# Dilated heads: the second score product contracts over 128 partitions instead of 64

## The chip, the cores and the metric

The kernel runs on one core of a Trainium2 chip. The metric is the device time of one execution in microseconds (us). Before the change three runs gave a median of 1386.52 us (1386.37 to 1387.81).

## What is computed

Two layers of a bidirectional encoder over 512 tokens of width 1024. Each layer mixes tokens with 16 heads of width 64: 4 differential heads, 6 dilated heads and 6 two-dimensional neighbourhood heads; their outputs go through an output projection, then a gated conv-MLP. The part that the change touches is the score of the dilated heads:

```
s = jnp.einsum('...nqd,...nkd->...nqk', qb, kb).astype(jnp.float32) * (DH ** -0.5)
s = jnp.where(mask, s, NEG)
```

The kernel computes all 512 x 512 scores of a head at once and puts the three dilation patterns into one additive table.

## The kernel before

Matrix products run in a 32-bit format (`F32R`) of reduced precision. For full precision a tensor is split into a rounded part `hi` and a remainder `lo`, and a projection is three products, hi*hi + lo*hi + hi*lo (`mm3`, lines 482 to 485; the value projections do the same on lines 684 to 686). Weights come from HBM as `raw` tiles (line 329), ScalarE (ACT) casts `hi` (line 351), and GpSimd (POOL) or VectorE (DVE) subtracts to get `lo` (line 353). Three such weight units fit during attention.

For a pair of dilated heads the rotary step writes hi and lo of q and k to a scratch tensor in HBM, and `dil_stack` (line 645) loads them back, stacked on the partitions, by seven DMAs of the SP queue (lines 651 to 657):

- `K[:, hh]`: 64 partitions hold k hi, 64 hold k lo (hi is the lower half for head 0 of the pair, the upper half for head 1)
- `Q[:, hh]`: q hi on both halves
- `L`: q lo of head 0 on partitions 0 to 63, q lo of head 1 on partitions 64 to 127

`dil_step` (line 931) computes a block of 128 queries of one head. Line 938 is a product over all 128 partitions, q hi with k hi plus q hi with k lo. Line 939 adds q lo with k hi: a product over 64 partitions only, `L[lr]` with `K[lr]`. Then DVE adds the table and takes the row minimum of the negated scores (line 942), ACT takes the exponential (line 947), DVE the reciprocal (line 951), ACT scales (line 952), TensorE (PE) transposes in four pieces (line 813, `tr` in `tr_stage`), ACT and DVE split the transposed block (lines 817 and 821), and PE multiplies with the values (lines 834 and 836). The differential heads run before them: their scores are line 902, DVE row maxima line 904, the combination of two probability blocks line 920, and they share lines 813 to 847. In layer 0 DVE also computes the modulation vectors (line 411), one row of weights at a time.

What sets the order: `attention_phase` runs a loop in which a generator (`proj`) emits two products' worth of projection at a time, a clock (`ck`) starts the later stages of the steps after given lags, and a credit counter lets a new step in. On top of that the framework's scheduler orders each engine's instructions by its own estimates when the program is built, so that a change of one shape can move neighbours. On the chip every engine runs its list in order.

There are 6 heads x 4 blocks x 2 layers = 48 executions of `dil_step`, so 48 products of line 938 and 48 of line 939.

Of the kernel before, what the change touches and what calls it, by code (L numbers as in the profile page):

```python
# [13 lines left out]
F32R = mybir.dt.float32r  # L14
# [8 lines left out]
S = 512  # L23
# [150 lines left out]
def build(ctx, tc, a):  # L174
    nc = tc.nc
    V, A, G, PE, SY = nc.vector, nc.scalar, nc.gpsimd, nc.tensor, nc.sync
# [11 lines left out]
    def uid():  # L188
        cnt[0] += 1
        return cnt[0]  # L190
# [4 lines left out]
    def tmp(shape=(128, 512), dt=F32, tag="tmp", bufs=TMP_BUFS):  # L195
        return wp.tile(list(shape), dt, tag=tag, bufs=bufs, name=f"{tag}{uid()}")
# [106 lines left out]
    def take(tag, shape=(128, 512)):  # L303
        assert av[tag] > 0, tag
        av[tag] -= 1
        return tmp(shape) if tag == "tmp" else ps(tag, shape)

    def give(tag):
        av[tag] += 1
# [258 lines left out]
    def attention_phase(l, gen, fest):  # L568
# [7 lines left out]
        def at(shape, dt, tag, bufs):  # L576
            return ap.tile(list(shape), dt, tag=tag, bufs=bufs, name=f"{tag}{uid()}")

        def mark(lag, *keys):
            ck.after(lag, lambda: ready.update(keys))  # L580
# [64 lines left out]
        def dil_stack(p):  # L645
            sv = scr["b", p].rearrange("(q v) r n -> q r v n", q=2)
            K = at([128, 2, S], F32R, "ks", 2)
            Q = at([128, 2, S], F32R, "qs", 2)
            L = at([128, S], F32R, "ql", 2)
            Kf, Qf, Lf = K.bitcast(F32), Q.bitcast(F32), L.bitcast(F32)  # L650
            SY.dma_start(Kf[:, 0], sv[1, :, 0])
            SY.dma_start(Kf[0:64, 1], sv[1, 64:128, 1])
            SY.dma_start(Kf[64:128, 1], sv[1, 0:64, 1])
            SY.dma_start(Qf[0:64], sv[0, 0:64])
            SY.dma_start(Qf[64:128], sv[0, 0:64])
            SY.dma_start(Lf[0:64], sv[0, 64:128, 0])
            SY.dma_start(Lf[64:128], sv[0, 64:128, 1])
            stk["b", p] = (K, Q, L)
            mark(2, ("b", p))

# [136 lines left out]
        def tr_need(st, qb):  # L797
            if qb % 2 == 0:
                return {"pt": 1, "ph": 1}
            return {"pt": 1, "if": lambda: ("ph", qb // 2) in st}  # L800

        def tr_stage(st, qb, P_of):
            half = qb // 2

            def tr():
                if ("ph", half) not in st:
                    av["ph"] -= 1
                    st["ph", half] = at([128, 4, 256], F32R, "ph", 2)
                    st["pl", half] = at([128, 4, 256], F32R, "pl", 2)
                pt = take("pt", (128, 4, 128))  # L810
                P = P_of()
                for kt in range(4):
                    PE.transpose(pt[:, kt], P[:, kt * 128:kt * 128 + 128], ident)  # L813
                give("tmp")
                st["pt", qb] = pt
                sl = slice((qb % 2) * 128, (qb % 2) * 128 + 128)
                A.copy(st["ph", half][:, :, sl], pt)  # L817

            def lo():
                sl = slice((qb % 2) * 128, (qb % 2) * 128 + 128)  # L820
                V.tensor_tensor(out=st["pl", half][:, :, sl], in0=st["pt", qb],  # L821
                                in1=st["ph", half][:, :, sl].bitcast(F32), op=ALU.subtract)
                st["lo", qb] = True
                give("pt")

            return tr, lo

        def av_half(st, half, vt, hidx, c, hh, fin):
            if half == 0:
                st["o"] = take("o")  # L830
            o = st["o"]
            oh = o[:, half * 256:half * 256 + 256]
            for kt in range(4):
                PE.matmul(oh, vt[:, kt, hidx, :], st["ph", half][:, kt], start=(kt == 0), stop=False)
            for kt in range(4):
                PE.matmul(oh, vt[:, kt, hidx, :], st["pl", half][:, kt], start=False, stop=(kt == 3))
            give("ph")
            if half == 1:
                if c not in of:
                    of[c] = at([128, S], F32, "of", 5)  # L840
                t = tmp()
                dst = slice(64 * hh, 64 * hh + 64)
                oth = slice(64 - 64 * hh, 128 - 64 * hh)
                A.copy(t[dst], o[oth])

                def s1():
                    V.tensor_tensor(out=of[c][dst], in0=o[dst], in1=t[dst], op=ALU.add)
                    give("o")
                    if fin:
                        fin()  # L850

                ck.after(1, s1)
# [78 lines left out]
        def dil_step(hd, qb, st):  # L931
            p, hh = divmod(hd, 2)
            K, Q, L = stk["b", p]
            lr = slice(64 * hh, 64 * hh + 64)
            nm = tmp((128, 2), tag="sm2", bufs=24)
            s = take("s")
            sl = slice(qb * 128, qb * 128 + 128)
            PE.matmul(s, Q[:, hh, sl], K[:, hh], start=True, stop=False)
            PE.matmul(s, L[lr, sl], K[lr, hh], start=False, stop=True)  # L939
            P = take("tmp")  # L940
            e0 = OFF_T + 384 - 128 * qb
            V.tensor_tensor_reduce(out=P, in0=s, in1=cst[:, e0:e0 + S], op0=ALU.add, op1=ALU.min, scale=1.0,
                                   scalar=3e38, accum_out=nm[:, 0:1])
            give("s")

            def s1():
                A.activation(out=P, in_=P, func=AF.Exp, bias=nm[:, 0:1], scale=-1.0, accum_out=nm[:, 1:2])

            def s2():
                r = tmp((128, 2), tag="sm2", bufs=24)  # L950
                V.reciprocal(out=r[:, 0:1], in_=nm[:, 1:2])
                A.activation(out=P, in_=P, func=AF.Copy, scale=r[:, 0:1])

            tr, lo = tr_stage(st, qb, lambda: P)
            stages = [(1, {}, s1), (1, {}, s2), (2, tr_need(st, qb), tr), (1, {}, lo)]
            if qb % 2 == 1:
                fin = (lambda: ready.add("b_done")) if hd == HB - 1 else None
                stages.append((2, {"o": int(qb == 1), "if": lambda: ("lo", qb - 1) in st and (qb == 1 or "o" in st)},
                               lambda: av_half(st, qb // 2, vs["vb"], hd, 2 + p, hh, fin)))
            ck.chain(*stages)  # L960
# [88 lines left out]
        for hd in range(HB):  # L1049
            st = {}  # L1050
            if hd % 2 == 0:
                stacks.append((("scr", ("b", hd // 2)), 4 * HD + 4 * hd - (4 if hd == 0 else 8),
                               lambda hd=hd: dil_stack(hd // 2)))
            steps += [(1.5, {"s": 1, "tmp": 1}, (("b", hd // 2), "vb"),
                       lambda hd=hd, qb=qb, st=st: dil_step(hd, qb, st)) for qb in range(4)]
# [266 lines left out]

# [12 lines left out]
```

## Time and profile before

| what | value |
|---|---|
| median of 3 runs | 1386.52 us |
| span of the profiled execution | 1383.9 us |
| PE busy (x instructions) | 1328.0 us, 96% (x6992) |
| DVE busy | 896.2 us, 65% |
| ACT busy | 608.2 us, 44% |
| POOL busy | 177.8 us, 13% |
| chain that ended last: PE, DVE, DMA | 85%, 8%, 3% |
| mean busy share of 16 DMA engines | q1 46.3%, q10 0.4% |

The profiled execution has a span of 1383.9 us from the first to the last instruction; its own device time is not listed apart, and the median of the timed runs stands 2.6 us above the span. Matmuls are pipelined: the length that a row gives for one is the time until its last result, so what a matmul costs in a full queue is the distance from its start to the start of the next.

### The profile page before, as it was taken

Reading aid. Unit: us, or ns where it says so; the run is one execution under the profiler, and the core shown is the slowest. Engines: PE = TensorE matmul, PEld = TensorE weight load, DVE = VectorE, ACT = ScalarE, POOL = GpSimd, SP = SyncE. Lnnn points to the kernel's source line nnn. Section 1 sums busy time; section 2 is a strip of 40 time slices with the busy share of each in tenths; the row PEclk is TensorE's granted clock in tenths of the full one; section 3 lists DMA queues with packets and bytes.
Section 4 is the critical chain, followed back from the end, with each engine's and each line's share of the span. In section 5 each row is a group of like instructions: output and inputs, shape, how many; then the busy total and the mean of one; then the engine's idle time right before and its main releaser. Section 6 shows DMA issues by size and latency. Waiting matters only on the chain.

```text
span 1383.9 us, 18577 instructions
## 1 busy us (share of the span) xinstructions
PE 1328.0 (96%) x6992; PEld 1109.3 (80%) x6992; DVE 896.2 (65%) x1615; ACT 608.2 (44%) x1051; POOL 177.8 (13%) x116
## 2 busy tenths in 40 slices
PE   5887899999999999999998989999999999999997
PEld 4785678779988888888898867877898888888886
DVE  7968976977776666656675697466576434443443
ACT  3336487645543233223342667775445322332331
POOL 3732321003000000000113232200200000000002
PEclk9999999999999999999999999999999999999998
DMA  9565564644466666665523645142334323333211
GB/s 365 164 182 150 162 208 142 197 134 149 124 195 181 202 180 184 198 196 165 175 76 108 178 140 171 57 126 77 97 98 124 103 94 91 96 102 92 79 44 61
DMA packets 69262, 196.16 MB, mean 142 GB/s; under 512 B 7602, under 2 KB 12850, under 8 KB 69044
## 3 DMA queue, kind: packets, MB, share of 16 engines
q1 hardware_dynamic: 68448, 193.10, 46.3%
q10 hardware_dynamic: 724, 1.87, 0.4%
q8 instruction: 55, 0.90, 0.3%
q14 instruction: 35, 0.29, 0.1%
HBM read 180.78 MB, written 14.16 MB: 141 GB/s over the span
## 4 chain that ended last, share of the span: by engine, by line
PE 85%; DVE 8%; DMA 3%; POOL 2%; issue 1%; ACT 1%; POOLq 0%; SPq 0%; DVEq 0%; ACTq 0%
PE pr L483 12%; PE pr L485 12%; PE pr L484 11%; PE s L484 5%; PE s L485 5%; PE s L483 5%; PE pt L484 4%; PE pt L485 4%; PE pt L483 4%; PE pt L813 2%; PE o L485 2%; PE o L483 2%; PE o L484 2%; PE o L1027 2%; PE s L939 1%
## 5 line engine op out<-in xcount | busy, mean ns | idle before, releaser
L351 ACT CAST whi<-raw 128x1024 fp32r<-128x1024 f32 (+2 forms) x144 | 135.0, 938 | 268.8 <-PE pr L485 103.4
L353 DVE TENSOR_TENSOR wlo<-raw,whi 128x1024 fp32r<-128x1024 f32 (+2 forms) x101 | 111.2, 1101 | 94.9 <-ACT whi L351 94.1
L444 POOL TENSOR_TENSOR tmp<-tmp,tmp 128x256 f32<-128x256 f32 (+1 forms) x38 | 36.7, 966 | 892.5 <-ACT tmp L442 891.2
L351 ACT CAST fhi<-raw 128x1024 fp32r<-128x1024 f32 (+1 forms) x76 | 74.9, 985 | 143.9 <-PE pr L485 53.7
L411 DVE CUSTOM_DVE_ANT_0 tmp<-raw,cb,par 128x1024 bf16<-128x1024 f32 x80 | 106.8, 1336 | 41.6 <-DMA raw<-w_ada 41.5
L485 PE MATMUL pr<-h,whi 128*128 128x512 f32 (+1 forms) x330 | 121.9, 374 | 8.0 <-POOL h L479 7.6
L483 PE MATMUL pr<-h,whi 128*128 128x512 f32 (+1 forms) x330 | 125.9, 382 | 1.6 <-DVE tmp L596 0.7
L353 POOL TENSOR_TENSOR wlo<-raw,whi 128x768 fp32r<-128x768 f32 (+1 forms) x43 | 96.0, 2238 | 243.2 <-ACT whi L351 215.6
L484 PE MATMUL pr<-h,wlo 128*128 128x512 f32 (+1 forms) x330 | 123.1, 373 | 1.0 <-POOL wlo L353 1.0
L353 DVE TENSOR_TENSOR flo<-raw,fhi 128x1024 fp32r<-128x1024 f32 (+1 forms) x76 | 87.4, 1150 | 55.2 <-ACT fhi L351 54.4
L483 PE MATMUL pr<-h,fhi 128*128 128x512 f32 (+1 forms) x244 | 86.7, 357 | 0.0
L484 PE MATMUL pr<-h,flo 128*128 128x512 f32 (+1 forms) x244 | 86.5, 356 | 0.0
L485 PE MATMUL pr<-h,fhi 128*128 128x512 f32 (+1 forms) x244 | 85.5, 357 | 0.5 <-DVE h L479 0.5
L485 PEld LDWEIGHTS pr<-h,whi 128*128 128x128 f32 x330 | 62.1, 190 | 19.8 <-POOL h L479 9.5
L483 PEld LDWEIGHTS pr<-h,whi 128*128 128x128 f32 x330 | 62.7, 190 | 16.0 <-issue 4.1
L484 PEld LDWEIGHTS pr<-h,wlo 128*128 128x128 f32 x330 | 63.1, 191 | 9.7 <-POOL wlo L353 1.2
L1157 ACT ACTIVATE tmp<-tmp 128x512 f32<-128x512 f32 x44 | 27.6, 631 | 94.3 <-DVE tmp L1152 77.4
L821 DVE TENSOR_TENSOR pl<-pt,ph 128x512 fp32r<-128x512 f32 x80 | 54.4, 686 | 14.7 <-ACT ph L817 14.5
L904 DVE TENSOR_REDUCE sm<-s 128x1 f32<-128x512 f32 x64 | 43.0, 682 | 28.4 <-PE s L902 28.0
L813 PE MATMUL pt<-cst,tmp 128*128 128x128 f32 x320 | 48.6, 274 | 13.3 <-DVE tmp L920 11.0
L817 ACT CAST ph<-pt 128x512 fp32r<-128x512 f32 x80 | 46.7, 586 | 32.3 <-PE pt L813 31.2
L477 ACT ACTIVATE h<-tmp,mod,gsc 128x256 fp32r<-128x256 f32 (+1 forms) x58 | 35.3, 621 | 53.3 <-DVE tmp L474 52.5
(265 smaller groups left out, 3657.3 us busy)
## 6 DMA issues: line engine op xcount, KB each, us to landing
raw<-w SPq DMA_DIRECT2D x132, 512.0 KB
raw<-w_ada SPq DMA_DIRECT2D x80, 512.0 KB
raw<-w SPq DMA_DIRECT2D x72, 384.0 KB
araw<-w_ada SPq DMA_DIRECT2D x16, 512.0 KB
raw<-w SPq DMA_DIRECT2D x16, 320.0 KB
ks<-nab SPq DMA_DIRECT2D x12, 384.0 KB
scr0b<-nat SPq DMA_DIRECT2D x12, 256.0 KB
scr1b<-nat SPq DMA_DIRECT2D x12, 256.0 KB
```

Source lines behind the costliest of these rows:

```text
L351: A.copy(hi, r)
L353: (G if on_pool else V).tensor_tensor(out=lo, in0=r, in1=hi.bitcast(F32), op=ALU.subtract)
L411: V.tensor_tensor_reduce(out=junk, in0=r, in1=cb, op0=ALU.mult, op1=ALU.add, scale=1.0, scalar=par[:, OFF_B + l * 48 + j:OFF_B + l * 48 + ...
L444: self.last = self.eng.tensor_tensor(out=self.sq[0][:, sl], in0=self.sq[0][:, sl], in1=self.sq[m][:, sl], op=ALU.add)
L477: ins = A.activation(out=hi, in_=t, func=AF.Identity, scale=A_col, bias=sh_col)
L483: PE.matmul(out, wh, hh, start=first, stop=False)
L484: PE.matmul(out, wl, hh, start=False, stop=False)
L485: return PE.matmul(out, wh, hl, start=False, stop=last)
L813: PE.transpose(pt[:, kt], P[:, kt * 128:kt * 128 + 128], ident)
L817: A.copy(st["ph", half][:, :, sl], pt)
L821: V.tensor_tensor(out=st["pl", half][:, :, sl], in0=st["pt", qb], in1=st["ph", half][:, :, sl].bitcast(F32), op=ALU.subtract)
L904: V.tensor_reduce(out=nm[:, m:m + 1], in_=s, axis=AX.X, op=ALU.max, negate=True)
```

## The change

`L` becomes as large as `Q`: q lo of both heads, stacked twice on the partitions. Line 656 and line 657 load 64 partitions x 2 heads x 512 each, twice the bytes of before (256 KB instead of 128 KB per DMA). The second product takes all 128 partitions of `L` and `K`, so it adds q lo with k hi and also q lo with k lo, which was left out before. The scratch that the framework keeps for descriptors of DMAs issued by POOL shrinks to 4096, which leaves room for the larger `L`. One line is gone, so lines behind 934 have numbers lower by one in the changed kernel: its two products are lines 937 and 938, and the DVE step is line 941.

```
@@ -646,15 +646,15 @@
-            L = at([128, S], F32R, "ql", 2)
+            L = at([128, 2, S], F32R, "ql", 2)
...
-            SY.dma_start(Lf[0:64], sv[0, 64:128, 0])
-            SY.dma_start(Lf[64:128], sv[0, 64:128, 1])
+            SY.dma_start(Lf[0:64], sv[0, 64:128])
+            SY.dma_start(Lf[64:128], sv[0, 64:128])
@@ -931,12 +931,11 @@
-            lr = slice(64 * hh, 64 * hh + 64)
...
-            PE.matmul(s, L[lr, sl], K[lr, hh], start=False, stop=True)
+            PE.matmul(s, L[:, hh, sl], K[:, hh], start=False, stop=True)
@@ -1322,7 +1321,7 @@
-    nc = bacc.Bacc("TRN2", target_bir_lowering=False, num_devices=1)
+    nc = bacc.Bacc("TRN2", target_bir_lowering=False, num_devices=1, dynamic_dma_scratch_size=4096)
```

The scheduler moves a few instructions. On PE all moves lie in layer 0; in layer 1 PE's order is the same as before. Three places matter below.

The first is PE in layer 0, where the sixth dilated step (score `s_1800`) stands among products of a projection (`pr_1772`). `pt_1781` is the transpose of the third step. Before:

```order
L485 MATMUL pr_1772<-h_275,whi_1529 128x512
L938 MATMUL s_1800<-ks_1330,qs_1331 128x512
L939 MATMUL s_1800<-ks_1330,ql_1332 128x512
L483 MATMUL pr_1772<-h_311,whi_1529 128x512
L484 MATMUL pr_1772<-h_311,wlo_1530 128x512
L485 MATMUL pr_1772<-h_312,whi_1529 128x512
L483 MATMUL pr_1772<-h_352,whi_1529 128x512
L834 MATMUL o_1811<-ph_1694,vb_791 128x256 x4
L813 MATMUL pt_1781<-cst,tmp_1686 128x128 x4
```

And in the changed kernel, from a point nine projection products later:

```order
L485 MATMUL pr_1772<-h_394,whi_1529 128x512
L937 MATMUL s_1800<-ks_1330,qs_1331 128x512
L938 MATMUL s_1800<-ks_1330,ql_1332 128x512
L483 MATMUL pr_1772<-h_434,whi_1529 128x512
L834 MATMUL o_1811<-ph_1694,vb_791 128x256 x4
L836 MATMUL o_1811<-pl_1695,vb_791 128x256
L813 MATMUL pt_1781<-cst,tmp_1686 128x128 x4
```

The sixth step's scores, and with them the products with the values and the transpose of the third step, come behind more projection products (those of `h_352`, `h_353`, `h_393` and `h_394`) than before.

The second is DVE in layer 0, in the last differential steps, just ahead of the first dilated step. `tmp_1448` is what PE's transpose `pt_1535` reads; in the difference:

```order
 L904 TENSOR_REDUCE sm_1499<-s_1501 128x1
 L919 SCALAR_TENSOR_TENSOR sm_1491<-sm_1491,sm_1156,nl_735 128x1
+L904 TENSOR_REDUCE sm_1499<-s_1505 128x1
+L920 SCALAR_TENSOR_TENSOR tmp_1448<-tmp_1448,sm_1491,tmp_1444 128x512
+L821 TENSOR_TENSOR pl_1473<-pt_1474,ph_1472 128x4x128
 L411 ISA tmp_1495,mod_99<-raw_1387,cb,par 128x1024
 L411 ISA mod_99 128x1
-L920 SCALAR_TENSOR_TENSOR tmp_1448<-tmp_1448,sm_1491,tmp_1444 128x512
-L904 TENSOR_REDUCE sm_1499<-s_1505 128x1
-L821 TENSOR_TENSOR pl_1473<-pt_1474,ph_1472 128x4x128
 L847 TENSOR_TENSOR of_1488<-o_1370,tmp_1489 64x512
```

The modulation row (line 411) goes behind the three instructions that PE and ACT wait for; the work in this stretch is the same.

The third is the SP queue in layer 1, at the load of the second pair of dilated heads (`ks_7797`, `qs_7798`, `ql_7799`); `raw_7872` is a weight unit of 768 columns:

```order
-L329 DMA raw_7872<-w 128x768
+L653 DMA ks_7797<-scr1b_7575 64x512
 L651 DMA ks_7797<-scr1b_7575 128x512
 L652 DMA ks_7797<-scr1b_7575 64x512
-L653 DMA ks_7797<-scr1b_7575 64x512
 L654 DMA qs_7798<-scr1b_7575 64x2x512
 L655 DMA qs_7798<-scr1b_7575 64x2x512
-L656 DMA ql_7799<-scr1b_7575 64x512
-L657 DMA ql_7799<-scr1b_7575 64x512
+L656 DMA ql_7799<-scr1b_7575 64x2x512
+L657 DMA ql_7799<-scr1b_7575 64x2x512
+L329 DMA raw_7872<-w 128x768
```

The weight unit now stands behind the seven loads of the stack instead of ahead of them.

## Rows read from the trace of the kernel before

**Rows 1.** Page, part 1: busy time and share of PE, PE's weight loads, and the others

```profile
PE 1328.0 (96%) x6992; PEld 1109.3 (80%) x6992; DVE 896.2 (65%) x1615; ACT 608.2 (44%) x1051; POOL 177.8 (13%) x116
```

**Rows 2.** PE's waits, whole span: who waited for whom; total, times, longest (us)

```profile
PE pt L813 <- DVE tmp L920: 11.0, 9, 1.9
```

**Rows 3.** Windows: length, busy us (count) of each engine, PE's granted clock, DMA share, GB/s

```profile
130.00:172.00 42.00, 35.43 (x179) 26.78 (x178) 41.23 (x67) 22.49 (x47) 13.82 (x6) 1.00 0.51 142
172.00:250.00 78.00, 78.00 (x420) 62.10 (x421) 55.48 (x132) 61.01 (x117) 13.82 (x7) 1.00 0.56 166
250.00:706.00 456.00, 455.66 (x2338) 381.30 (x2336) 315.52 (x546) 171.90 (x272) 22.44 (x22) 1.00 0.58 174
832.00:848.00 16.00, 16.00 (x79) 11.76 (x78) 15.43 (x31) 11.59 (x23) 2.84 (x1) 1.00 0.59 174
```

**Rows 4.** Lines 938 and 939: count, ns min/median/max, first and last start, shapes

```profile
L938 PEld LDWEIGHTS s<-ks,qs x48: 186/188/192, 166.6 to 913.3; 128*128 128x128 f32 x48
L938 PE MATMUL s<-ks,qs x48: 387/397/505, 166.8 to 913.5; 128*128 128x512 f32 x48
L939 PE MATMUL s<-ks,ql x48: 491/492/502, 167.1 to 913.8; 64*128 64x512 f32 x48
```

**Rows 5.** PE's timeline at a dilated step among projections: start us, length us

```profile
244.73 0.40 PE L938 MATMUL s<-ks,qs 128*128 128x512 f32 x1
245.06 0.49 PE L939 MATMUL s<-ks,ql 64*128 64x512 f32 x1
245.48 0.50 PE L483 MATMUL pr<-h,whi 128*128 128x512 f32 x1
245.82 0.39 PE L484 MATMUL pr<-h,wlo 128*128 128x512 f32 x1
246.05 0.40 PE L485 MATMUL pr<-h,whi 128*128 128x512 f32 x1
```

**Rows 6.** PE's timeline, a step behind transposes and ahead of value projections

```profile
206.69 0.48 PE L938 MATMUL s<-ks,qs 128*128 128x512 f32 x1
207.10 0.50 PE L939 MATMUL s<-ks,ql 64*128 64x512 f32 x1
207.53 0.45 PE L684 MATMUL pr<-whi,h 128*128 128x384 f32 x1
207.81 0.34 PE L685 MATMUL pr<-wlo,h 128*128 128x384 f32 x1
207.99 0.35 PE L686 MATMUL pr<-whi,h 128*128 128x384 f32 x1
```

**Rows 7.** PE's timeline, a transpose that waited, then full-array products

```profile
171.98 0.63 PE L813 MATMUL pt<-cst,tmp 128*128 128x128 f32 x4 [0.44 <-DVE tmp L920]
172.37 0.48 PE L484 MATMUL pr<-h,wlo 128*128 128x512 f32 x1
172.69 0.39 PE L485 MATMUL pr<-h,whi 128*128 128x512 f32 x1
```

**Rows 8.** ACT's timeline, layer 1: scaling of the second dilated step (line 952)

```profile
843.32 0.69 ACT L952 ACTIVATE tmp<-tmp,sm 128x512 f32<-128x512 f32 x1
```

**Rows 9.** PE's timeline, layer 1: first and fourth step, transposes of the second

```profile
832.58 0.39 PE L938 MATMUL s<-ks,qs 128*128 128x512 f32 x1
...
841.37 0.39 PE L938 MATMUL s<-ks,qs 128*128 128x512 f32 x1
...
844.53 0.60 PE L813 MATMUL pt<-cst,tmp 128*128 128x128 f32 x4
```

**Rows 10.** Window at the border of the two layers, columns as in Rows 3

```profile
758.00:764.60 6.60, 5.31 (x17) 5.31 (x18) 1.24 (x2) 0.83 (x1) 0.51 (x2) 0.50 0.78 235
```

**Rows 11.** Timeline of POOL and DVE in layer 0, ahead of the dilated steps

```profile
160.12 2.64 POOL L353 TENSOR_TENSOR wlo<-raw,whi 128x1024 fp32r<-128x1024 f32 x1 [9.54 <-ACT whi L351]
160.46 2.85 DVE L920 SCALAR_TENSOR_TENSOR tmp<-tmp,sm,tmp 128x512 f32<-128x512 f32 x1
```

**Rows 12.** Line 656 on the SP queue, layer 1: issue ns, first and last start

```profile
L656 SPq DMA_DIRECT2D ql<-scr1b x3: 603/605/612, 814.0 to 861.2; - x3
```

## The prediction

> **What bounds the kernel now.** First the busy shares of the page: PE is busy 96% of the span, DVE 65%, ACT 44% [rows 1]. A share says little about a single stage, so next PE's waits: the longest of them in total is the transpose of a differential step waiting for DVE, 11.0 us in 9 waits [rows 2]. It shows that DVE does end PE's waits somewhere. The windows show where [rows 3]: in 130 to 172 us, the differential steps of layer 0 and the first dilated ones, DVE is busy 41.23 of 42.00 us and PE only 35.43; in 172 to 250, where the rest of layer 0's dilated steps stand, PE is busy all 78.00 us and DVE 55.48. Layer 1 begins in the same way: DVE 15.43 of 16.00 in 832 to 848. Behind layer 0's steps PE goes on without a break, 455.66 of 456 us. So time taken from PE's list in the dilated steps comes off the end, except where DVE, not PE, sets the pace; that is the case in the first steps of each layer.
>
> Then the two products themselves. Line 939 takes 492 ns in the median, line 938 only 397, though the first feeds half as many partitions and both stream 512 columns [rows 4]. The cost in a full queue is the distance from start to start, and there the whole effect is to be seen [rows 5]. From 938 to 939 it is 0.33 us, from 939 to the next product 0.42, from that to the one behind it 0.34; after that the full-array products go on at 0.23. Not only the 64-row product is dear: the one ahead and the one behind it pay too. All three have 128 columns of weights and a free result buffer, and no engine is named as a releaser in these rows. What differs is the shape 64*128 between two of 128*128.
>
> **The change, part by part.** *The product of line 939 becomes full-array.* Now, among projections, three products take 245.82 - 244.73 = 1.09 us [rows 5]. All full-array they should take 3 x 0.23 = 0.69 us, the pace of the last two rows there. That is 0.40 us less. Behind transposes and ahead of value projections the three take 207.81 - 206.69 = 1.12 us [rows 6]. Without the 64-row one I put 0.32 us for the first (a full-array product behind transposes, 172.37 to 172.69 [rows 7]), 0.23 for the second and 0.18 for a value product of 384 columns (207.81 to 207.99 [rows 6]): 0.73 us, 0.39 less. These two patterns agree, so I take 0.39 us for each of the 48 steps [rows 4]: 18.7 us off PE's list. It is a price by subtraction: no row shows the changed product itself, but the one ahead of it, line 938, has its shape, its kind of operands and 397 ns. From below the bound is nothing (the gaps stay, second rival), from above 0.40 x 48 = 19.2 us.
>
> Here a page speaks against the change. The Trainium skill, "TensorE: Matmul & The Clock Gate", section "Why this matters for your kernels", has a single product with a short contraction take the same time as a full one, the gain of small ones lying only in running several at once. By that rule widening the contraction changes nothing and the sum is 0 instead of 18.7 us; the trace does not agree, with 492 ns against 397 for the same 512 columns [rows 4].
>
> *What DVE keeps back.* In layer 0 two dilated steps stand ahead of the transpose at 171.98, which waits for DVE's line 920 [rows 7]. DVE is full up to there [rows 3], so what PE saves in these two it waits longer: 2 x 0.39 = 0.8 us lost. The next two steps' transposes have waits of their own to fear, since DVE also feeds the dilated steps, but the third step's transpose now stands behind the sixth step's scores and more projection products, which fill the time. I take nothing more there. In layer 1 PE's order is unchanged. The transpose of the second step starts at 844.53, and its input is done at 843.32 + 0.69 = 844.01: a slack of 0.52 us [rows 8, 9]. Four steps stand ahead of it (832.58 to 841.37), and they save 4 x 0.39 = 1.56 us; if DVE's chain stands still, 1.56 - 0.52 = 1.0 us of that becomes a wait. Bounds: nothing lost (DVE's chain moves along), or all of the first eight steps of both layers, 16 x 0.39 = 6.2 us.
>
> *The moved DVE and PE instructions in layer 0.* Line 920 for `tmp_1448` and two others go ahead of a modulation row. That may remove a PE wait near 163 us, but DVE's work up to the wait at 171.98 is the same, and that wait takes up what was won. I count 0. Its bound as a loss is one collision: line 920 there is stretched to 2.85 us beside a subtraction of POOL of 2.64 us [rows 11], so a DVE instruction that meets POOL at a bad moment can lose up to 2.6 us; as a gain the bound is the same, if the collision that is there now goes away.
>
> *Six pairs of loads twice as large.* Each stack brings 2 x 128 KB more, 262 KB, six stacks 1.6 MB. At the mean of 142 GB/s in that stretch [rows 3] 262 KB take 1.8 us. Issue on the SP queue is 0.6 us for the small load [rows 12], and I take the same for the large one, since the number of instructions stays. What hides it: in layer 1 the first `L` is issued at 814.0 us and the first product starts at 832.58, 18 us later [rows 12, 9]. If that cover were gone, PE would wait up to 1.8 us at each of six stacks. In layer 1 a weight unit moves behind seven loads of a stack; weights are fetched three units ahead, a unit is 24 projection products of 0.23 us or 5.5 us without the attention products between them, so some 16 us ahead. I count 0. The smaller descriptor scratch I count at nothing as well: no row of the trace shows a DMA issued by POOL, for which it is kept. The extra q lo times k lo comes free in the same pass.
>
> *The clock.* At the border of the layers, 758.0 to 764.6, the granted clock is 0.50, the 1.2 GHz level, and PE is busy only 5.31 of 6.60 us [rows 10]. At full clock this would take half, so such a stretch costs 2.6 us. In the stretches around the dilated steps it is 1.00, the 2.4 GHz level [rows 3]. Layer 1 starts some 8 us earlier now; whether the stretch stays is open, so 2.6 us goes into the range on either side. I count 0.
>
> **Sum.** 18.7 - 0.8 - 1.0 = 16.9 us. Against the profiled span: 1383.9 - 16.9 = 1367.0. The median of the runs lies 2.6 us above that span, so I give 1386.5 - 16.9 = **1369.6 us**.
>
> **Rivals.** *First, DVE holds on longer.* If it keeps back all of the first eight steps of each layer, 18.7 - 6.2 = 12.5 us remain: 1374.0. For it speaks DVE's full window [rows 3] and the collisions with POOL [rows 11], which a faster PE may set off elsewhere, as it frees weight buffers sooner; against it that from 172 us on PE is full and DVE has 22 us to spare.
>
> *Second, the shape is not the cause.* Then the three distances stay, and the time stays at 1386.5. For it: the trace has no other 64-row product of 512 columns to compare. Against it: no row without a 64-row product beside it shows 0.42 us, and the row ahead and the row behind both pay, which a slow read of `L` would not explain.
>
> *Third, slower: weight loads of the same rows come into the open.* A load takes 188 ns [rows 4]. If it could not run under a product of the same rows, each of the three products would cost 0.19 + 0.23 = 0.42 us, 48 x 3 x 0.42 = 60.5 us against 48 x 1.1 = 52.8 now: 7.7 us slower, 1394.2. It decides from 0.13 us of open load for each product on, where three cost 1.09. Against it: full-array products follow one another at 0.23 us [rows 5] with loads of 0.19, which leaves no room for an open load. The Trainium skill, "TensorE: Matmul & The Clock Gate", section "The mechanism", does say that a weight load overlaps with a product under way only when the row groups differ; by that rule this rival would come true, and the trace does not agree (0.23 us from start to start [rows 5]).
>
> **How the numbers follow.** The forecast has 0.74, from 1365.2 us (18.7 us and a vanished slow stretch, 1386.5 - 18.7 - 2.6) to the first rival's 1374.0. The first rival has 0.16, up to 1374.0 + 2.6 = 1376.6. Second rival, or the gain lost by something not seen here: 0.05. Third: 0.03. Below 1365.2: 0.02. The range is 1365.2 to 1376.6 and leaves out about 0.1 to 0.15. A measurement of this kernel can tell 0.2%, 2.8 us, from no change. Faster: 0.74 + 0.16 + 0.02 = 0.92; the same: 0.05; slower: 0.03.
>
> **What would show it.** The second product (line 938 in the changed kernel) with shape 128*128 and a median near 397 ns; from start to start 0.23, 0.23 and 0.23 us in the three, 0.32 for the first behind transposes. PE's total busy time down by 15 us or more; PE full and DVE at two thirds or more in the dilated steps. PE waits at the transposes of the first steps of each layer, some 1 us each in total. The prediction is wrong if the distances stay above 0.3 us, if new waits for DVE or ACT in the dilated steps sum to over 5 us, or if a wait for `ql` or `raw` shows up.

## The result, and the profile after

The changed kernel takes **1370.68 us** in the median of 4 runs (1368.71 to 1373.33), beside 1387.11 for the kernel before on the same chip. The ratio is 0.9886, with a 95% interval of 0.9874 to 0.9898; of 1386.52 us that is 15.8 us less, the gain that this text goes by (the two medians above are 16.4 us apart). Run once more, word for word, it gave 1368.82 us and 0.9883 (0.9868 to 0.9897). 0.9886 x 1386.5 is 1370.7, with the interval 1369.0 to 1372.4; the forecast was 1369.6, in a range of 1365.2 to 1376.6. The profiled execution has a span of 1370.5 us (1372.36 us as a run), 13.4 us under the span before.

Busy time by engine (page of the changed kernel, part 1), against [rows 1]:

```profile
PE 1310.2 (96%) x6992; PEld 1108.9 (81%) x6992; DVE 896.2 (65%) x1615; ACT 605.5 (44%) x1051; POOL 179.4 (13%) x116
```

PE has lost 17.8 us of busy time with the same number of instructions; DVE's is the same to the tenth. The two products by line (count, ns min/median/max, first and last start), against [rows 4]:

```profile
L938 PE MATMUL s<-ks,ql x48: 388/392/477, 168.1 to 901.2; 128*128 128x512 f32 x48
```

492 ns have become 392. The same step among projections, on PE's timeline, against [rows 5]:

```profile
240.38 0.39 PE L937 MATMUL s<-ks,qs 128*128 128x512 f32 x1
240.61 0.40 PE L938 MATMUL s<-ks,ql 128*128 128x512 f32 x1
240.84 0.39 PE L483 MATMUL pr<-h,whi 128*128 128x512 f32 x1
241.07 0.40 PE L484 MATMUL pr<-h,wlo 128*128 128x512 f32 x1
```

and one ahead of value projections and behind a transpose, against [rows 6]:

```profile
205.47 0.60 PE L813 MATMUL pt<-cst,tmp 128*128 128x128 f32 x4
205.82 0.48 PE L937 MATMUL s<-ks,qs 128*128 128x512 f32 x1
206.14 0.40 PE L938 MATMUL s<-ks,ql 128*128 128x512 f32 x1
206.97 0.41 PE L684 MATMUL pr<-whi,h 128*128 128x384 f32 x1 [0.44 <-DVE nat L738]
```

From start to start the first shows 0.23 us three times where 0.33, 0.42 and 0.34 stood, 0.69 us in place of 1.09; the second shows 0.32 where 0.41 stood. The last row of the second is a sign of the other side: there PE now waits 0.44 us for DVE. In the windows this looks as follows, against [rows 3] (the last is the border of the layers, against [rows 10]):

```profile
130.00:172.00 42.00, 36.25 (x186) 27.94 (x185) 40.76 (x68) 23.54 (x50) 13.95 (x6) 1.00 0.54 148
172.00:242.00 70.00, 67.93 (x402) 60.29 (x402) 55.40 (x128) 57.58 (x112) 15.80 (x7) 1.00 0.67 193
242.00:698.00 456.00, 455.73 (x2339) 381.58 (x2338) 314.68 (x546) 173.09 (x274) 21.34 (x21) 1.00 0.57 174
820.00:836.00 16.00, 15.29 (x79) 12.51 (x78) 16.00 (x31) 10.68 (x22) 4.95 (x2) 1.00 0.50 147
752.80:759.40 6.60, 5.44 (x17) 5.44 (x18) 1.10 (x2) 0.83 (x1) 0.51 (x2) 0.50 0.78 220
```

In 172 to 242 PE idles 2.1 us where it was full before, and at the head of layer 1 DVE is busy 16.00 of 16.00 us and PE idles 0.7. The stretch at the 1.2 GHz level is still there, only 5.2 us earlier.

**Where the time went** is read best step by step: the start of a step's first product before, less the start of the same step's after. A step that keeps its whole gain adds 0.39 to the difference (taken from the starts before rounding).

```
step    before   after   difference
1       166.80  167.73   -0.93
3       174.53  175.33   -0.80
10      199.69  197.51    2.17
11      204.46  203.95    0.50
12      206.69  205.82    0.87
13      211.17  210.66    0.51
24      246.97  242.22    4.76
25      832.58  827.30    5.28    (layer 1)
27      838.91  832.82    6.08
28      841.37  835.76    5.61
29      846.36  840.70    5.66
48      913.50  900.98   12.52
```

From step 13 to 24 it grows by 4.25 in 11 steps, from 29 to 48 by 6.86 in 19: 0.39 and 0.36 a step. Layer 0 as a whole gives 6.1 us (-0.93 to 5.15 behind step 24), layer 1 gives 7.6 (5.28 to 12.92), of 24 x 0.39 = 9.4 each. What was kept back stands in a few places. Where two steps should have brought 0.78, the first two brought 0.13; from step 10 to 11 the difference falls by 1.67 and from 12 to 13 by 0.36, where each step should have brought 0.39; in layer 1 it falls by 0.47 from 27 to 28 and all but stands still to 29, a loss of 1.2 in all. These places make up 4.7 of the 5.1 us by which the two layers stay behind their 18.8. (The 0.93 us at the start arose before the first dilated step; more on it at the end.)

The place at step 10, on PE's timeline and then on DVE's:

```profile
197.51 0.39 PE L937 MATMUL s<-ks,qs 128*128 128x512 f32 x1
199.41 0.63 PE L813 MATMUL pt<-cst,tmp 128*128 128x128 f32 x4 [1.50 <-DVE pl L821]
199.79 0.48 PE L938 MATMUL s<-ks,ql 128*128 128x512 f32 x1
```

```profile
195.68 1.28 DVE L411 CUSTOM_DVE_ANT_0 tmp<-raw,cb,par 128x1024 bf16<-128x1024 f32 x1 [1.70 <-DMA raw<-w_ada]
196.89 0.08 DVE L411 DVE_READ_ACCUMULATOR2_ANT mod<- 128x1 f32 x1
196.89 1.18 DVE L738 SCALAR_TENSOR_TENSOR nat<-pr,nat 128x512 fp32r<-128x512 f32 x1
197.99 0.67 DVE L847 TENSOR_TENSOR of<-o,tmp 64x512 f32<-64x512 f32 x1
198.59 0.67 DVE L821 TENSOR_TENSOR pl<-pt,ph 128x512 fp32r<-128x512 f32 x1
```

To be read backwards: PE waits 1.50 us for line 821, which stands on DVE behind a modulation row (line 411), and that row waited 1.70 us for its weights from the DMA queue on which the stack loads run too. By the SP queue's timeline its weights were issued at 185.60 us; the doubled loads of the second stack were issued at 196.40 and 197.05, when the row had begun, so they did not delay it. The place at step 28, PE, DVE and POOL:

```profile
835.76 0.50 PE L937 MATMUL s<-ks,qs 128*128 128x512 f32 x1 [0.70 <-DVE sm L941]
```

```profile
832.28 0.68 DVE L821 TENSOR_TENSOR pl<-pt,ph 128x512 fp32r<-128x512 f32 x1
832.88 2.21 DVE L603 TENSOR_TENSOR tmp<-tmp,tmp 128x512 f32<-128x512 f32 x1
835.02 0.68 DVE L941 CUSTOM_DVE_ANT_0 tmp<-s,cst 128x512 f32<-128x512 f32 x1
```

```profile
832.14 2.40 POOL L353 TENSOR_TENSOR wlo<-raw,whi 128x1024 fp32r<-128x1024 f32 x1 [6.12 <-DMA raw<-w]
```

Line 603, which takes 0.67 us on DVE at 829.09, takes 2.21 beside POOL's subtraction of 832.14, and ends 0.55 us behind it (832.88 + 2.21 = 835.09 against 834.54). Line 941, which frees the score buffer, comes behind it, and PE waits 0.70 us. In run one below, which has the same order with the old shape, POOL is later in relation to DVE's list and hits line 615, for which PE does not wait (so it was in the kernel before, at 839.33 us):

```profile
839.17 2.28 DVE L615 TENSOR_TENSOR nat<-tmp,nat 128x512 fp32r<-128x512 f32 x1
```

The Trainium skill, "SBUF — State Buffer", section "SBUF: two separate sides", says that DVE and GpSimd have one pair of ports in common, which a DVE instruction with two inputs in SBUF, as line 603 has, and a GpSimd one that reads SBUF hold to their end, one at a time; these rows agree with it, 2.21 us against 0.67.

### The profile page after: what moved, and what is told of

Same layout as the page of the kernel before. It is cut to its first block, busy times and chain, and to the rows that moved or that the text cites. A ratio compares the mean times of both kernels' runs of the same rounds, so it can differ in the third digit from the quotient of the medians.

```text
span 1370.5 us, 18584 instructions
## 1 busy us (share of the span) xinstructions
PE 1310.2 (96%) x6992; PEld 1108.9 (81%) x6992; DVE 896.2 (65%) x1615; ACT 605.5 (44%) x1051; POOL 179.4 (13%) x116
## 4 chain that ended last, share of the span: by engine, by line
PE 81%; DVE 10%; DMA 4%; POOL 2%; issue 2%; ACT 1%; SPq 0%; POOLq 0%; DVEq 0%; ACTq 0%
PE pr L483 11%; PE pr L485 11%; PE pr L484 11%; PE s L484 5%; PE s L485 5%; PE s L483 5%; PE pt L485 4%; PE pt L484 4%; PE pt L483 4%; PE pt L813 2%; PE o L485 2%; PE o L483 2%; PE o L484 2%; PE o L1026 2%; DVE sm L904 1%
## 5 line engine op out<-in xcount | busy, mean ns | idle before, releaser
L353 DVE TENSOR_TENSOR wlo<-raw,whi 128x1024 fp32r<-128x1024 f32 (+2 forms) x101 | 111.0, 1099 | 93.8 <-ACT whi L351 92.9
L411 DVE CUSTOM_DVE_ANT_0 tmp<-raw,cb,par 128x1024 bf16<-128x1024 f32 x80 | 109.1, 1364 | 46.5 <-DMA raw<-w_ada 46.2
```

The costliest lines, as they stand in the source:

```text
L353: (G if on_pool else V).tensor_tensor(out=lo, in0=r, in1=hi.bitcast(F32), op=ALU.subtract)
L411: V.tensor_tensor_reduce(out=junk, in0=r, in1=cb, op0=ALU.mult, op1=ALU.add, scale=1.0, scalar=par[:, OFF_B + l * 48 + j:OFF_B + l * 48 + ...
```

## The experiments

Theory: the 64-row product costs because PE goes over from 128 rows to 64 and back, 0.39 us each time, and the change removes just that. (A visit is a run of 64-row products between full-array ones, a border the place where PE goes over.) Rivals: the loads or the order, which the change also moves, carry the gain or take a part of it back; or it is the number of rows in itself that is paid for.

**One: only the shape undone.** Loads, scratch and the order on every engine stay those of the changed kernel.

```
-            PE.matmul(s, L[:, hh, sl], K[:, hh], start=False, stop=True)
+            lr = slice(64 * hh, 64 * hh + 64)
+            PE.matmul(s, L[lr, hh, sl], K[lr, hh], start=False, stop=True)
```

> The changed kernel with its loads, its descriptor scratch and its order of instructions on every engine, but the second product again over 64 partitions. If the shape is the cause, the whole gain goes: 1385 to 1389 us, the level of the kernel before, with 0.42 us behind the 64-row product. If order or loads made the gain, it stays near 1371 us. Halfway, 1377 to 1382, would mean that both have a share.

Measured: 1385.34 us (10 runs), 0.9993 (0.9983 to 1.0003) of before. By the count of the lines (busy us, mean ns) the second product is as dear as before:

```profile
L939 PE MATMUL s<-ks,ql 64*128 64x512 f32 x48 | 23.8, 495 | 0.0
```

So the doubled loads, the other order and the smaller scratch are together worth nothing that can be measured, and the whole gain is the shape.

**Two: the same rows in two visits, and a control.** Each step's score is made in two halves of 256 columns, so that PE goes over to 64 rows twice in a step; the control has the same halves over 128 rows.

```
+            lr = slice(64 * hh, 64 * hh + 64)
+            for c in (slice(0, 256), slice(256, 512)):
+                PE.matmul(s[:, c], Q[:, hh, sl], K[:, hh, c], start=True, stop=False)
+                PE.matmul(s[:, c], L[lr, hh, sl], K[lr, hh, c], start=False, stop=True)
```

> Each dilated step has two 64-row products of 256 columns, each between full-array products, in place of one of 512; columns and results are those of the kernel before, and the visits to the 64-row shape are 96 in place of 48. If each visit costs 0.39 us, the time rises by up to 48 x 0.39 = 18.7 us over the split full-array control of the same call plus the 18.7 us of the first visits: control + 33 to 40 us, some 1405 us. If the 64-row product is slow for each column that it streams, the columns are the same and the time stays near the kernel before: 1385 to 1390 us.

> Control for the run with two visits: the same split into four products of 256 columns, all over 128 partitions. If splitting costs nothing (0.12 us for 256 columns, as in the products with the values, 0.23 for 512), 1369 to 1375 us, the changed kernel's level. If weight loads come into the open with shorter products, 0.07 us for each of 192 products, up to 13 us more.

Measured: 1403.56 us, 1.0124 (1.0108 to 1.0141), and the control 1374.15, 0.991 (0.9895 to 0.9925). The two have the same order on every engine. The difference is 29.4 us for 96 visits, 0.31 us each. That is under the 33 to 40 expected, but with the columns unchanged the price has gone from some 15 us (run one against the changed kernel, 1385.34 - 1370.68) to 29. PE's timeline in the two-visit kernel shows how it is spread:

```profile
245.19 0.36 PE L939 MATMUL s<-ks,qs 128*128 128x256 f32 x1
245.49 0.38 PE L940 MATMUL s<-ks,ql 64*128 64x256 f32 x1
245.80 0.38 PE L939 MATMUL s<-ks,qs 128*128 128x256 f32 x1
246.11 0.38 PE L940 MATMUL s<-ks,ql 64*128 64x256 f32 x1
246.42 0.50 PE L483 MATMUL pr<-h,whi 128*128 128x512 f32 x1
```

Between products of different rows the distance is 0.30 or 0.31 us for 256 columns; products of that size and of one shape follow one another at 0.12 (run six below).

**Three: 96 rows.** The last quarter of the partitions is left out of the second product, so a part of the low products is missing.

```
-            PE.matmul(s, L[:, hh, sl], K[:, hh], start=False, stop=True)
+            PE.matmul(s, L[0:96, hh, sl], K[0:96, hh], start=False, stop=True)
```

> The second product over partitions 0 to 95 only (its last quarter is left out), the order of all instructions is that of the changed kernel. If it is the row tile of 64 that costs, 96 rows fill the whole array's shape and the time is the changed kernel's, 1368 to 1374 us. If the cost follows the number of rows that are left idle, half of the gain goes: 1377 to 1381 us.

Measured: 1372.43 us, 0.9895 (0.9875 to 0.9915), the changed kernel's time within the intervals. 96 rows cost what 128 cost:

```profile
L938 PE MATMUL s<-ks,ql 96*128 96x512 f32 x48 | 19.1, 397 | 0.0
```

So it isn't that every product of fewer rows is paid for; of the sizes tried, 64 is and 96 isn't.

**Four: no second product at all** (the term with q lo is left out), to see what the full-array one still costs.

```
-            PE.matmul(s, Q[:, hh, sl], K[:, hh], start=True, stop=False)
-            PE.matmul(s, L[:, hh, sl], K[:, hh], start=False, stop=True)
+            PE.matmul(s, Q[:, hh, sl], K[:, hh], start=True, stop=True)
```

> The changed kernel without the second product: q lo is left out of the dilated scores. If a full-array product costs its 0.23 us and no more, 48 x 0.23 = 11.0 us go from PE's list; without those of the first eight steps of each layer, where DVE sets the pace, 32 x 0.23 = 7.4. So 1360 to 1364 us. If the second product still had a hidden cost of a switch (0.4 us and more), 1350 to 1355; if PE were not the bound behind the first steps, 1368 and more.

Measured: 1362.46 us, 0.9823 (0.9809 to 0.9838), 8.2 us under the changed kernel, 0.17 a step where PE's list has 0.23. Taken from the kernel before, leaving the product out would have won about 24 us, of which the new shape alone already gives 16.

**Five: do modulation rows on DVE keep the gain back?** In both kernels the rows of layer 0's modulation, which come between the steps, start later.

```
-            if l == 0 and nst % 4 == 0 and si >= 10 and ada_st["n"] < 40:
+            if l == 0 and nst % 4 == 0 and si >= 28 and ada_st["n"] < 40:
```

> The kernel before with layer 0's modulation rows on DVE held back until the twelfth dilated step, so that DVE has some 10 us less work in the stretch in which it sets the pace. If DVE sets the pace there, PE's waits for it in layer 0's first steps shrink: 1380 to 1385 us. If not, 1385 to 1388.

> The changed kernel with the same shift of modulation rows. If DVE kept back the gain of layer 0's first ten steps (1.6 us won where 10 x 0.39 = 3.9 was to be had), the start of the tenth step moves against the kernel e5_late_before by close to 3.9 us, and the gain between the two is 17 to 19 us. If something else kept it back (loads, order), the steps' gain stays near 1.6 and the whole near 15 to 16.

Measured: 1393.53 us, 1.0049 (1.0032 to 1.0066), for the kernel before so altered, and 1378.08, 0.9937 (0.9922 to 0.9952), for the changed one. A miss: both are some 7 us slower. PE's waits in the stretch behind layer 0's steps tell why (260 to 700 us, of the altered changed kernel):

```profile
PE pr L483 <- DVE x L1098: 3.3, 3, 2.1
PE pr L483 <- ACT h L477: 1.4, 2, 0.9
PE pr L485 <- DVE h L479: 1.1, 1, 1.1
```

The rows are needed for the residual of line 1098 (1099 in the other kernel), and come too late for it; unaltered, the stretch has 0.3 us of such waits in both kernels. The gain between the two is 15.45 us, what it is without the shift. To the start of the tenth step the difference grows by 1.7 us (from -1.40 to 0.30) where 3.5 was due: by the test set above, something other than the rows keeps the gain back, and it goes at other steps, from the fourth to the fifth and from the sixth to the seventh. Step by step layer 0 now gives 7.2 us of 9.4 in place of 6.1, but the second execution of the unaltered changed kernel gives 7.6 (against run one's trace), so the rows can't be said to be what holds it back.

**Six: the same change to the neighbourhood heads**, whose score products are 64-row ones too: q is copied into zero-padded tiles, so that they run over 128 rows.

```
+                G.memset(zf[64:128, 0], 0.0)
+                G.memset(zf[0:64, 1], 0.0)
+                SY.dma_start(zf[0:64, 0], src[0:64].bitcast(F32))
+                SY.dma_start(zf[64:128, 1], src[64:128].bitcast(F32))
...
-                PE.matmul(s[:, i], qh[hr, sl], kh[hr, kw], start=True, stop=False)
+                PE.matmul(s[:, i], qh[:, hh, sl], kh[:, kw], start=True, stop=False)
```

> The changed kernel, and the neighbourhood heads' score products (64 partitions, 144 of them in 30 visits in the trace) over all 128 as well: q of a pair is copied by DMA into two tiles in which the other head's half is zero; zeros by POOL. If each visit costs 0.39 us, however many products it has, 30 x 0.39 = 11.7 us go: 1357 to 1361 us. If the copies are late or POOL's zeros hold up DVE, a part is given back: 1362 to 1368. If the 64-row products of 256 columns cost nothing extra, 1370 or more.

Measured: 1364.18 us, 0.9841 (0.9825 to 0.9856): faster than both kernels, 6.5 us under the changed one. The same visit on PE's timeline, in the changed kernel

```profile
927.97 0.66 PE L1009 MATMUL pt<-cst,tmp 128*128 128x128 f32 x4
928.55 0.38 PE L980 MATMUL s<-nat,nat 64*128 64x256 f32 x1
928.77 0.28 PE L981 MATMUL s<-nat,nat 64*128 64x256 f32 x1
928.89 0.27 PE L982 MATMUL s<-nat,nat 64*128 64x256 f32 x1
...
929.24 0.27 PE L982 MATMUL s<-nat,nat 64*128 64x256 f32 x1
929.44 0.50 PE L483 MATMUL pr<-oh,whi 128*128 128x512 f32 x1
929.78 0.39 PE L484 MATMUL pr<-oh,wlo 128*128 128x512 f32 x1
```

and in this run:

```profile
922.27 0.66 PE L1023 MATMUL pt<-cst,tmp 128*128 128x128 f32 x4
922.68 0.36 PE L994 MATMUL s<-nat,qs 128*128 128x256 f32 x1
...
923.36 0.28 PE L996 MATMUL s<-nat,ql 128*128 128x256 f32 x1
923.47 0.39 PE L483 MATMUL pr<-oh,whi 128*128 128x512 f32 x1
923.70 0.39 PE L484 MATMUL pr<-oh,wlo 128*128 128x512 f32 x1
```

From the transpose to line 484 it is 1.81 us with 64 rows and 1.43 with 128: 0.38 us for a visit of six products. Within the visit the products follow at 0.12 us in both. So a visit is paid for once, going in and coming out, however many products it has. There are 30 visits in the changed kernel, some 11 us of them; 6.5 arrived. Summed over all of them, from the instruction ahead to the second one behind, the visits took 38.3 us, and their products now take 31.8 (in 31 stretches, as one is split in two). Three of these are drawn out by waits of PE for DVE at scores and transposes: 0.42 us at 244.60, 0.27 and 0.44 from 261.77 on, 0.48 at 901.72. That is 1.6 of the 4.9 us that are missing (30 x 0.38 less 6.5); the rest is not accounted for, since this run also moves PE's order there.

**Seven: are the doubled loads free?** The changed kernel once more, and a form whose second product is full-array but whose q lo is loaded once, into one half of `L`, with zeros in the other.

```
-            SY.dma_start(Lf[0:64], sv[0, 64:128])
-            SY.dma_start(Lf[64:128], sv[0, 64:128])
+            G.memset(Lf[64:128, 0], 0.0)
+            G.memset(Lf[0:64, 1], 0.0)
+            SY.dma_start(Lf[0:64, 0], sv[0, 64:128, 0])
+            SY.dma_start(Lf[64:128, 1], sv[0, 64:128, 1])
```

> The changed kernel once more, word for word, beside the next two runs, since its runs so far spread over 4.6 us. Expected: 1368.5 to 1373.5 us, median 1370 to 1372. If the first median was a lucky one, 1373 or more.

> The second product stays full-array, but q lo is loaded once, as before the change, and the other half of L is set to zero on POOL (two fills of some 0.53 us for each of six stacks). If the doubled loads cost something, by way of the modulation row that comes 1.70 us late behind them and the 1.5 us that PE then waits at a transpose, the time is 1 to 2 us below the changed kernel's: 1368.5 to 1370. If they are hidden, as the prediction counted them, it is the changed kernel's time within 1 us; if the fills hold up DVE or the stack loads, 1 to 3 us above it.

Measured: 1368.82 us for the repeat, 1370.96 with 0.9892 (0.9878 to 0.9907) for the zero half. The zero half has the order of the kernel before on PE, DVE, ACT and SP, and the loads of before in bytes and number; what the engines do in addition are twelve fills on POOL. So it says two things. Beside the kernel before, 1386.10 us here, it is a second test of the shape alone: the full-array product wins some 15 us in the old order and with the old loads as well. Beside the changed kernel, half the loads and the old order together don't make it faster, though DVE waits less for modulation weights in all, 37.7 us in place of 46.5 in the repeat (idle time ahead of line 411). In the repeat's trace the row of step 10 comes only 0.25 us late, and the 1.50 us wait of PE isn't there:

```profile
195.21 1.28 DVE L411 CUSTOM_DVE_ANT_0 tmp<-raw,cb,par 128x1024 bf16<-128x1024 f32 x1 [0.25 <-DMA raw<-w_ada]
```

But the wait is no single event either. The row is late by 1.75 us in the trace of run three and by 1.54 in the control of run two, with PE waits of 1.6 and 1.5 us for line 821 as in the changed kernel; by 1.12 us in run four, 0.63 in the zero half, 0.30 in run six. It is on time in the kernel before, with two visits, and in run one, which has the doubled loads too, and in run eight. So it goes with the faster PE, and by how much differs between executions; no run shows that the loads cost time. Whether the zero half's fills on POOL do (2.1 us, with overlapping intervals) stays open.

**Eight: both together**, zero half and neighbourhood heads.

> Zero half of L for the dilated heads together with the neighbourhood heads' products over 128 rows (as in the run e6_na_full, 1364.2 us). A candidate that has no 64-row score product left in dilated or neighbourhood heads. Expected: 1362.5 to 1364.5 us if the doubled loads cost 0 to 1.5 us; above 1365 if twelve more fills on POOL collide with DVE.

Measured: 1365.89 us, 0.9862 (0.9845 to 0.9878). Not better than run six; the miss is in the direction of the fills, but 1.7 us with overlapping intervals do not show that they are its cause. Run six stays the fastest that computes all terms.

## Why the prediction was right, point by point

- *0.39 us a step.* Right. The undisturbed distances are 0.22 to 0.23 us and 0.32 behind transposes, the steps from 29 to 48 win 0.36 each and those from 13 to 24 0.39, and PE's busy time fell by 17.8 us of the 18.7 forecast. That the two neighbours of the 64-row product pay too, read from [rows 5], was the point: the price of line 939 alone, 492 - 397 ns, would have given 4.6 us. The second rival (the shape is not the cause) fell with run one: by its interval, 2.4 us (0.0017 x 1386) at most are the rest of the change's.
- *What DVE keeps back, 0.8 + 1.0 us.* The mechanism was right, the size too small. In the first two steps of layer 0 0.7 us went, as forecast. The place forecast for layer 1, the second step's transposes, was wrong: the loss of 1.2 us there comes at step 28, from line 603's collision with POOL. That 1.2 lies so near the 1.0 of the sum is chance. Not foreseen in "I take nothing more there": the wait of the value projection behind step 12 for line 738 (0.44 us; with the gain that was due, 0.75 in all), which the repeat's trace has as well (0.42), and, in the profiled execution but not in the repeat, the wait of 1.50 us behind the row that came late at step 10. By the traces 9.4 - 6.1 and 9.4 - 7.6, 5.1 us in all, were kept back in the profiled execution, and 9.4 - 7.6 in layer 0 of the repeat. By the medians it is 18.7 less 15.8 or 16.2, 2.5 to 2.9 us against 1.8. So this is the term that was mis-sized, by about 1 us in the medians and 3 in the profiled execution; the range was wide enough for it.
- *First rival (DVE holds 6.2 us back, 1374.0).* It didn't come true in the medians, though the 5.1 us of the profiled execution come near its 6.2. From step 13 and from step 29 on the steps kept 0.39 and 0.36 us each.
- *Third rival (weight loads come into the open).* False, and for the reason given: full-array products of the same rows follow at 0.22 to 0.23 us. It is the old form that had weight loads in the open, at its two borders (last section).
- *Six doubled loads at nothing.* Right in the total (runs one and seven), and PE shows no wait for `ql`. The modulation rows, which come by the same queue, were left out; one was late by up to 1.75 us, though in the changed kernel's trace the doubled loads of the second stack were issued only behind it (step 10 above).
- *Moved instructions at nothing.* Right within the same 2.4 us.
- *The clock.* In the profiled execution the stretch at 1.2 GHz stayed as long as it was (5.44 us of PE in 6.60, before 5.31), and nothing was won or lost by it. In the repeat, behind the same wait of PE for DVE (3.84 us, line 707), it was shorter: the granted clock is 0.50 in the stretch shown here and 1.00 behind it.

```profile
753.90:757.30 3.40, 3.40 (x11) 3.40 (x12) 0.00 (x0) 0.00 (x0) 0.00 (x0) 0.50 0.99 284
```

  Against run one the repeat wins 1.0 us more than a step's gain from step 24 to step 25, the profiled execution 0.4. So the 2.6 us kept for this in the range were not needed, but the term is not the same in every execution.

## What to carry to other kernels

Between products of different row counts look at the distances from start to start, not at the duration of the odd one: the neighbours pay most of it. A 64-row product alone among full-array ones is worth padding or stacking to 128 rows wherever the extra rows come from a load with cover or can be zeros (run seven); if it must stay, put all 64-row products that are ready into one visit, since the price is for going in and out. Then ask which engine paces the first steps of a stage, since what PE saves there it only waits longer.

## What was not expected of the hardware

The price is that of the two borders, and not of the product: about 0.19 us each, in single products of 512 columns, in halves of 256 and in visits of six, and 96 rows have none. What a border holds shows in PE's weight loads (PEld), before, in the step of [rows 5], and then in the changed kernel, in the same step:

```profile
244.50 0.19 PEld L938 LDWEIGHTS s<-ks,qs 128*128 128x128 f32 x1
245.05 0.18 PEld L939 LDWEIGHTS s<-ks,ql 64*128 64x128 f32 x1 [0.36 <-issue]
245.48 0.19 PEld L483 LDWEIGHTS pr<-h,whi 128*128 128x128 f32 x1 [0.24 <-issue]
```

```profile
240.38 0.19 PEld L938 LDWEIGHTS s<-ks,ql 128*128 128x128 f32 x1
```

Among full-array products a load runs under the product ahead: that of line 938 starts at 240.38 us, its product at 240.61. At a border it does not: the load for the 64-row product starts at 245.05, with its own product (245.06), and so does the next (245.48, both). A load of 0.18 to 0.19 us in the open at each border is about the price of a border. How much of the price is the load, and how much the wait until the product ahead is through (line 939 starts 0.10 us later than at full pace), these rows don't tell apart.

The Trainium skill, "TensorEngine Tiling (Array Packing)", section "Key Properties", says that changing the tiling mode drains TensorE. The rows agree in that the price hangs on the change and not on the number of products (0.38 us for a visit of six, 0.39 for one of one), and give it a size; that a drain is all of it they don't show.

The stretch ahead of the first dilated step, in which nearly the same work stands, differs by 0.9 us between the profiled executions of before and after, and by 2.2 us between run one and the repeat. The clock may have a part in it: over the first 165 us the mean granted clock was 0.98 in run one, 0.97 in the changed kernel and 0.96 in the repeat, whose first dilated steps start at 166.46, 167.73 and 168.70 us; the kernel before, 0.96 and 166.80, does not fit that order, so the cause stays open. The difference alone is as large as the terms of DVE in the sum, so those can't be told from a median, only step by step.
